# Layer 0 front: modulation products, value weights, value tiles and token sums placed differently

## The chip, the cores and the metric

The kernel runs on one core of a Trainium2 chip. The metric is device time in microseconds of one execution. The kernel is one straight program of 20932 profiled instructions; all five engines (TensorE or PE, VectorE or DVE, ScalarE or ACT, GpSimd or POOL, and SyncE or SP, which issues most transfers) work at once and meet by semaphores.

## What is computed

A two-layer encoder trunk on 1024 tokens of width 1024. Layer 0 is differential attention, layer 1 latent attention. Cut to what matters here:

```python
shift, scale, gate = split(silu(c) @ ada_w + ada_b)          # per layer: the modulation
h = rmsnorm(x, norm_g) * (1 + scale) + shift
q, k, v, z = split(h @ w_in0)                                 # layer 0, 8 heads
q, k = rope(q), rope(k)
p = softmax(q1 @ k1.T) - lam * softmax(q2 @ k2.T)
o = rmsnorm(p @ v, subln_g) * (1 - lam0) * silu(z)
x = x + gate * (o @ w_out0)
```

The modulation of layer 1 (shift and scale) depends on `c` alone, so its products can be done at any time before layer 1.

## The kernel before, in words

Float32 products are made from three matmuls: every operand is split into a rounded high part (a cast on ACT) and the rest (a subtraction on POOL or DVE), and `mm3` adds high*high, high*low and low*high in one accumulator. A weight block has 128 rows by 512 columns. All lines are those of the profile.

The front of layer 0 runs as follows.

1. The tokens are normalised, transposed and modulated into `h0`, first half, then second half (`h_chunk`, lines 519 and 782 to 793), and the value columns of heads 0 to 3 are made beside it. In the second half's loop, steps k = 1 to 4 each run one *modulation product* of layer 1: `mod_load` (L475) fetches 512 KB of weights, `mod_dot` (L480) multiplies by `c2` and sums along the row, on DVE. There are 16 such products: `MODS_K` (4) here, `sum(MODS)` (8) among the later value tiles, and the rest in attention 0.
2. `combos0` (L941 to L984) forms sums and differences of `h0`, the *token sums*, in 18 steps: additions on DVE, then a split into `TK` (cast on ACT L948, subtraction on DVE L949). Its last five steps make the fourth combination (L979, L980) and finish the splits. The steps hang on `side`, a list from which one entry is run at each tick, that is after each group of three matmuls; `None` is an empty tick. Beside it TensorE makes the second half of key and query strip 0 and gate strip 0 (`z_done`, whose output L851 frees the strip's accumulator).
3. For heads 2, 4 and 6 (`FRONT`), `z0_pair` makes a key strip and a query strip together with seven products instead of eight. Weights are fetched by `z0_fetch` (L932) a pair ahead, combined on DVE (L993 to L996) and split (`split_z`). After each output, `late(p, i)` starts work that belongs to what follows. In the last pair it fetches eight value weight blocks (`fetch_v1`, L1070, four and four) and splits them into `wv1` (`split_v1`, L1077 and L1078). Buffers: `zraw` has six, `zt` has twelve; both are freed by what last used them.
4. The first strip of `ORDER0` follows (`stream0.step(Z_PRE)`), then eight value tiles of heads 4 to 7 (`v0_tile`, "vps" in the profile). Each is stored with `store_v` (L418, L419, L421) from one of 16 `tk` buffers of the pool `tp`. Before tile `V_LATE` (6) attention begins with the first query tile.
5. Then `tp` is closed, and the pool `a0b` (the exponentials `e`, the transposed probabilities `pt`, the value tiles `vt`) takes its memory: each new tile waits for what lay there before.

Attention 0 goes over 8 heads, each in 8 query tiles (`q_tile`, `after_scores`). `stream0` fills TensorE with strips for later heads, and after each query tile `gate_step0` advances `gate_steps0` by one *slot*: its products (modulation, then eight for the gate) use two buffers `ada` of the pool `pg`. `rot_done` and `z_done` put a rotation's steps on `side`: `first_` and `second` on POOL, an empty tick, then `high` (cast on ACT, L398) and `low` (POOL).

The order on each engine is set by a planner at build time. It takes the program's order as priority and hoists instructions whose inputs and buffers it expects to be ready; some are tied by hand (`issue_after`, `keep_in_program_order`). Each engine and each queue then runs in that order.

Of the kernel before, what the change touches and what calls it, by code (L numbers as in the profile page):

```python
# [38 lines left out]
ROT = 2  # L39
# [4 lines left out]
Z_PRE = 16  # L44
V_LATE = 6
MODS = (2, 2, 2, 2, 0, 0, 0, 0)
MODS_K = 4
V1_AT = (3, 3)
NORM_AT = 5
PRE0 = (0, 0, 0, 0, 1, 2, 2, 3, 2, 2, 2)  # L50
# [3 lines left out]
FRONT = (2, 4, 6)  # L54
# [25 lines left out]
def f32v(ap):  # L80
    return ap.bitcast(F32)
# [3 lines left out]
def trunk(ctx: ExitStack, tc: tile.TileContext, A, out):  # L85
# [229 lines left out]
    side = Side()  # L315
# [100 lines left out]
    def store_v(l, sp, acc, tt, fh, tag="vst", bufs=None):  # L416
        v = sp.tile([P, 2, HF], F32R, name="tk" if tag == "tk" else "v_hl", tag=tag, bufs=bufs or VB[l])
        store_v.act = S.copy(v[:, 0, :], acc).ins  # L418
        V.tensor_sub(v[:, 1, :], acc, f32v(v[:, 0, :]))  # L419
        th, tl = tt // 4, tt % 4  # L420
        SP.dma_start(  # L421
            vS[l][fh][:, th, :, :, tl, :].rearrange("h p l d -> p l h d"),
            f32v(v).rearrange("p l (h d) -> p l h d", h=4),
        )

    def load_v(vp, l, h, ths=(0, 1)):
        vt = []
        for th in ths:
            t = vp.tile([P, 2, 4, P], F32R, name="vt", tag="vt", bufs=3)
            SP.dma_start(f32v(t), vS[l][h // 4][h % 4, th])  # L430
            vt.append(t)
        return vt
# [57 lines left out]
    def mod_job(n):  # L490

        j, i = divmod(n, 2)
        _, bsh, bsc, a_, b_ = mods[1]
        bias, acc = ((bsh, b_), (bsc, a_))[i]
        return A["ada_ss1"][j, i], bias[:, j : j + 1], acc[:, j : j + 1]

    def gen_mods(load, c2):

        for n in range(sum(MODS) + MODS_K):
            src, bias, acc = mod_job(n)  # L500
# [52 lines left out]
    pg = pool(stG, "pg")  # L553
# [228 lines left out]
    for k in range(KT + SKEW1):  # L782
        if k < KT:
            if 0 < k <= MODS_K:
                next(mods_g)
# [11 lines left out]
    def v0_tile(tt, fh, wv):  # L797
        half, tl = tt // 4, tt % 4
        acc = bank("acc", "vps")
        c_ = slice(tl * P, (tl + 1) * P)  # L800
        for k in range(KT):
            hh, hl = h0[k][half]
            mm3(acc, hh[:, c_], hl[:, c_], wv[k][0], wv[k][1], k == 0, k == KT - 1)
            side.tick()
        store_v(0, tp, acc, tt, fh, "tk", 16)


    KS, QS, GZ = {}, {}, {}
# [10 lines left out]
    def rot_done(kind, h):  # L819
        def f(acc, half):  # L820
            raw = wp.tile([P, HF], F32, name="rp_raw", tag="rp", bufs=6)
            if kind:
                S.copy(raw, acc)
            else:
                S.mul(raw, acc, SC0)
            fetch, *steps = rot_job(kind, h, half, G, raw)
            fetch()
            side.add(*[None] * ROT, *steps[:2], None, *steps[2:4])
        return f

    def load_k(h):
# [15 lines left out]
    def z_done(h):  # L847
        def f(acc, half):
            t = wp.tile([P, HF], F32, name="zth", tag="rp", bufs=6)
            S.activation(t, acc, AF.Tanh, scale=0.5)  # L850
            V.scalar_tensor_tensor(out=t, in0=t, scalar=1.0, in1=acc, op0=ALU.add, op1=ALU.mult)  # L851
            SP.dma_start(zS[h, half], t)
            if parked:
                fetch, *steps = rot_job(*parked.pop(0), G)
                side.add(fetch, None, None, *steps[:2], None, *steps[2:4])
        return f

    def load_gate(h, half):
# [58 lines left out]
    tp = pool(stT0, "tp", side="right")  # L917
# [8 lines left out]
    def zrt(name):  # L926
        return zp.tile([P, HF], F32, name=name, tag="zraw", bufs=6)

    def z0_fetch(p, parts):
        for m, f in parts:  # L930
            raw = zt("zraw") if p else zrt("zraw")
            SP.dma_start(raw, A["w_s0"][1 - m, FRONT[p], f])  # L932
            zraw.append(raw)
# [4 lines left out]
    def zt(name):  # L938
        return zp.tile([P, HF], F32, name=name, tag="zt", bufs=12)
# [124 lines left out]
    wv1 = []  # L1064
    wvraw = []

    def fetch_v1(n):
        for _ in range(n):
            raw = zrt("wvr")
            SP.dma_start(raw, A["w_v0"][len(wv1) + len(wvraw), 1])  # L1070
            wvraw.append(raw)

# [9 lines left out]
    zw = z0_weights()  # L1082
    zq = []
    cg = combos0()
    for _ in range(18):
        side.add(lambda: next(cg), None)
    for _ in gen_half(wk0, h0, 1, lambda acc: park(1, 0, 1.0)(acc, 1)):
        side.tick()
    wz0 = split_strip([(t, 4) for t in z0raw])
# [10 lines left out]
    def late(p, i):  # L1100
        if p + 1 < len(FRONT):
            if i < 2:
                z0_fetch(p + 1, ((i, 0), (i, 1)))
            return
        if i == 0:
            pre.extend(raw_of(*ORDER0[0], f) for f in range(2))
        if i == 1:
            fetch_v1(4)
        if i == 2:
            for _ in range(2):  # L1110
                for a, b in zip(w1, split_raw(pre.pop(0), 4)):
                    a += b
            split_v1(4, V)
            fetch_v1(4)
        if i == 3:
            split_v1(4, G)

# [63 lines left out]
    a0b = pool(st2b, "a0b")  # L1181
    for n, nb in (("osq", 4), ("o", 2)):
        a0b.tile([P, HF], F32, name=n, tag=n, bufs=nb)

# [89 lines left out]
            if kh == 1 and qp % 2 == 1:  # L1276
                c["close"](qp // 2, c["o_"], self.zz)

    tails, hooks, VT = [None, None], [], {}

    def run_tails(fill):

# [76 lines left out]
    def gate_steps0():  # L1359

        gcol = sm.tile([P, KT], F32, name="gcol", tag="gcol", bufs=1)
        yield
        w = []
        jobs = [mod_job(n) for n in range(sum(MODS) + MODS_K, 2 * KT)]
        late = len(jobs)
        jobs += [(A["ada_g0"][j], part("ada_bg0")[:, j : j + 1], gcol[:, j : j + 1]) for j in range(KT)]
        for n in range(len(jobs)):
            while len(w) < min(2, len(jobs) - n):
                with tc.issue_after(mod_load.last):
                    w.append(mod_load(jobs[n + len(w)][0], pg, 2))  # L1370
            yield
            if n >= late and (n - late) % 2 == 0:
                yield
            with behind("V"):
                mod_dot(w.pop(0), *jobs[n][1:], c2)
                if n == late - 1:
                    g, _, _, a_, _ = mods[1]
                    V.scalar_tensor_tensor(out=a_, in0=a_, scalar=1.0, in1=g, op0=ALU.add, op1=ALU.mult)
        SP.dma_start(gateS[0].rearrange("(p j) -> p j", p=P), gcol)
        yield  # L1380
        SP.dma_start(c2, gateS[0][None, :].to_broadcast([P, D]))
        gb = c2[:, :HF], c2[:, HF:]

        def two(name):
            t = pg.tile([P, D], F32, name=name, tag="ada", bufs=2)
            return t[:, :HF], t[:, HF:]

        def put(*pairs):
            for n, t in pairs:
                SP.dma_start(tS[0][n, h], t)  # L1390

        for h in range(4):
            b_ = (b11, b12), (b21, b22) = two("ob1"), two("ob2")
            for m in range(2):
                for f in range(2):
                    SP.dma_start(b_[m][f], A["w_out0"][f, 4 * m + h])
                yield
            for m in range(2):
                for f in range(2):
                    in_turn(G.tensor_mul(b_[m][f], b_[m][f], gb[f]))  # L1400
                if m:
                    put((0, b11))
                yield
            put((1, b21), (4, b22))
            in_turn(G.tensor_sub(b12, b12, b11))
            t2 = a0c.tile([P, HF], F32, name="ot2", tag="ot2", bufs=2)
            in_turn(G.tensor_sub(t2, b22, b12))
            yield
            put((3, b12), (2, t2))
            in_turn(G.tensor_sub(b11, t2, b11))  # L1410
            in_turn(G.tensor_sub(b21, b21, t2))
            yield
            put((5, b11), (6, b21))
            yield
        for h, wait in ((0, 46), (1, 54)):
            while slot0 < wait:
                yield
            a_ = (a11, a12), (a21, a22) = two("oa1"), two("oa2")
            for m in range(2):
                for f in range(2):  # L1420
                    SP.dma_start(a_[m][f], oF[0][h + 4 * f, m])
                yield
            for _ in combine(a11, a12, a21, a22):
                yield
            SP.dma_start(sS[0][0, h], a22)
            SP.dma_start(sS[0][2, h], a21)
            yield
            SP.dma_start(sS[0][1, h], a11)
            SP.dma_start(sS[0][3, h], a12)
            yield  # L1430
# [36 lines left out]
    class Seven:  # L1467
# [40 lines left out]
        def fetch(self, n):  # L1508
            for h in range(4):
                self.fetch_a(n, h)  # L1510
                self.fetch_w(n, h)
# [13 lines left out]
    class Pre2:  # L1525
        n = 0
# [304 lines left out]
    for n, rows, acc, f in ((3, 4, Z, 1), (4, 0, Z, 1), (5, 4, Y, 1), (6, 4, Y, 0)):  # L1831
# [5 lines left out]
        for i in range(4):  # L1837
# [24 lines left out]
            if i == 1 and n == 5:  # L1862
                raws = [[], []]
                with tc.issue_after(w6):
                    for k, (tag, nb) in enumerate((("wraw", 2), ("gz", 3))):
                        for f in range(2):
                            raw = wst.tile([P, HF], F32, name="wraw", tag=tag, bufs=nb)
# [796 lines left out]
    for tiles, a, b in LAST1:  # L2664
        acc = {i: bank("z", "oyb") if a else Y[i] for i in tiles}
# [87 lines left out]
```

## Time and profile before

| | us |
|---|---|
| median of 3 runs (lowest, highest) | 1413.85 (1412.5, 1414.33) |
| the profiled execution | 1414.53 |
| its span, first to last instruction | 1412.7 |
| PE busy | 1368.7 |
| DVE busy | 999.6 |
| ACT busy | 736.7 |
| POOL busy | 716.5 |

In rows of a timeline the first number is the start in us from the span's start, the second the length in us, followed by engine, line, operation, the tile written, the tiles read, and a count; a bracket at the end tells how long the engine had been idle and whom it waited for. In rows of waits stand the waiting engine, tile and line, whom it waited for, the total in us, how many times, and the longest.

### The profile page before, as it was taken

How to read it: one execution, taken by the hardware profiler on the slowest of the kernel's cores; microseconds unless marked ns; L12 is line 12 of the kernel's file. 1: busy time of each engine (PE TensorE's matmuls, PEld its weight loads, DVE VectorE, ACT ScalarE, POOL GpSimd, SP SyncE). 2: the span in 40 equal slices, each digit the busy share in tenths (PEclk: the TensorE clock that was granted, in tenths of full speed). 3: DMA queues.
4: the chain of work that ended last, by engine and by line, in shares of the span. 5: the costliest groups of instructions: out<-in, count | busy, mean ns of one | idle time of the engine just before them, and what ended most of it. 6: DMA issues, size and time to landing. Idle time of an engine off the chain costs nothing.

```text
span 1412.7 us, 20932 instructions
## 1 busy us (share of the span) xinstructions
PE 1368.7 (97%) x7298; PEld 1144.2 (81%) x7298; DVE 999.6 (71%) x1414; ACT 736.7 (52%) x1332; POOL 716.5 (51%) x574
## 2 busy tenths in 40 slices
PE   8998889899999999999999999999999999999997
PEld 6786678788888888887787788887888888888886
DVE  7799726899877878788687986545656655555684
ACT  5534313556666556566756543335444454445554
POOL 4434441466688776454785233433141273844673
PEclk9999999999999999999999999999999999999999
DMA  9854788786878787756584236399434354665473
GB/s 338 280 172 156 247 227 258 222 241 192 256 236 245 222 246 223 226 163 202 161 290 155 79 106 221 124 299 265 148 107 117 107 181 147 196 218 198 147 258 120
DMA packets 175243, 282.41 MB, mean 200 GB/s; under 512 B 23457, under 2 KB 60449, under 8 KB 175138
## 3 DMA queue, kind: packets, MB, share of 16 engines
q1 hardware_dynamic: 168610, 266.40, 60.8%
q10 hardware_dynamic: 4608, 8.39, 1.6%
q0 software_dynamic: 1920, 6.29, 1.1%
q8 instruction: 57, 0.93, 0.3%
q14 instruction: 48, 0.39, 0.1%
HBM read 182.49 MB, written 86.98 MB: 191 GB/s over the span
## 4 chain that ended last, share of the span: by engine, by line
PE 68%; DVE 11%; DMA 6%; issue 5%; ACT 4%; POOL 4%; SPq 2%; POOLq 0%; ACTq 0%; DVEq 0%
PE s L2367 8%; PE tr L439 6%; PE s L1155 6%; PE acc L180 6%; PE acc L179 6%; PE acc L178 6%; PE pv L178 3%; PE pv L180 3%; PE pv L179 3%; DVE ada L480 2%; PE vps L178 1%; PE vps L180 1%; PE vps L179 1%; PE oy L179 1%; PE oy L180 1%
## 5 line engine op out<-in xcount | busy, mean ns | idle before, releaser
L442 DVE TENSOR_TENSOR ptl<-tr,pth 128x512 fp32r<-128x512 f32 x256 | 176.1, 688 | 148.9 <-ACT pth L441 144.4
L441 ACT CAST pth<-tr 128x512 fp32r<-128x512 f32 x256 | 150.3, 587 | 249.8 <-PE tr L439 243.5
L456 DVE TENSOR_REDUCE nm<-s 128x1 f32<-128x1024 f32 x192 | 233.6, 1217 | 22.1 <-PE s L1155 13.0
L224 POOL TENSOR_TENSOR wl<-wraw,wh 128x512 fp32r<-128x512 f32 (+2 forms) x65 | 85.3, 1314 | 250.2 <-ACT wh L223 182.6
L458 ACT ACTIVATE e<-s,nm 128x1024 f32<-128x1024 f32 x128 | 143.4, 1120 | 52.0 <-DVE nm L456 50.1
L439 PE MATMUL tr<-ident,e 128*128 128x128 f32 x1024 | 156.0, 274 | 8.3 <-DVE ptl L442 7.8
L439 PEld LDWEIGHTS tr<-ident,e 128*128 128x128 f32 x1024 | 121.0, 141 | 49.4 <-DVE ptl L442 25.6
L178 PE MATMUL pv<-pth,vt 128*128 128x256 f32 x512 | 147.5, 288 | 0.0
L179 PE MATMUL pv<-ptl,vt 128*128 128x256 f32 x512 | 146.8, 287 | 0.0
L180 PE MATMUL pv<-pth,vt 128*128 128x256 f32 x512 | 144.6, 282 | 0.0
L178 PE MATMUL acc<-h0h,wh 128*128 128x512 f32 x264 | 109.8, 416 | 3.4 <-ACT wh L223 3.4
L180 PE MATMUL acc<-h0h,wl 128*128 128x512 f32 x264 | 105.7, 401 | 4.6 <-POOL wl L224 4.6
L179 PE MATMUL acc<-h0l,wh 128*128 128x512 f32 x264 | 104.8, 397 | 0.0
L178 PEld LDWEIGHTS pv<-pth,vt 128*128 128x128 f32 x512 | 97.5, 190 | 2.9 <-ACT pth L441 0.2
L179 PEld LDWEIGHTS pv<-ptl,vt 128*128 128x128 f32 x512 | 97.5, 190 | 2.5
L180 PEld LDWEIGHTS pv<-pth,vt 128*128 128x128 f32 x512 | 97.5, 190 | 0.5
L1503 POOL TENSOR_TENSOR wol<-wol,woh 128x512 fp32r<-128x512 f32 x56 | 82.4, 1495 | 25.4 <-ACT woh L1502 23.8
L1155 PE MATMUL s<-ks,qa 128*128 128x512 f32 x256 | 85.4, 414 | 5.1 <-DVE e L1163 4.9
L1163 DVE SCALAR_TENSOR_TENSOR e<-s,z,e 128x1024 f32<-128x1024 f32 x64 | 82.2, 1284 | 2.0
L1155 PE MATMUL s<-ks,qb 128*128 128x512 f32 x256 | 83.1, 400 | 0.0
L458 ACT ACTIVATE s<-s,nm 128x1024 f32<-128x1024 f32 x64 | 70.1, 1095 | 6.6 <-DVE nm L456 6.6
L224 POOL TENSOR_TENSOR wl<-zraw,wh 128x512 fp32r<-128x512 f32 (+2 forms) x32 | 42.8, 1346 | 50.5 <-ACT wh L223 50.5
(494 smaller groups left out, 3612.5 us busy)
## 6 DMA issues: line engine op xcount, KB each, us to landing
ada<-in_ada_ss SPq DMA_DIRECT2D x32, 512.0 KB, 5.6
vt<-vS SPq DMA_DIRECT2D x32, 512.0 KB, 5.0
wol<-tS SPq DMA_DIRECT2D x56, 256.0 KB, 5.3
wraw<-in_w_s SPq DMA_DIRECT2D x52, 256.0 KB, 3.8
vS<-v_hl SPq DMA_DIRECT2D x24, 512.0 KB, 5.8
tS<-ob SPq DMA_DIRECT2D x48, 256.0 KB, 3.7
bc_s<-bc_d SPq DMA_DIRECT2D x34, 256.0 KB, 4.1
hS<-rp_sw ACTq DMA_DIRECT2D x32, 256.0 KB, 4.8
```

Of the source, the lines that this page charges most:

```text
L178: PE.matmul(psum, ah, bh, start=first, stop=False, skip_group_check=skip)
L179: PE.matmul(psum, ah, bl, start=False, stop=False, skip_group_check=skip)
L180: mm3.last = PE.matmul(psum, al, bh, start=False, stop=last, skip_group_check=skip).ins
L224: sub = (V if pair_of else G).tensor_sub(l_[:, :n], raw[:, :n], f32v(h_[:, :n]))
L439: transpose_p.last = PE.transpose(tr[:, j, :], p[:, kt * P : (kt + 1) * P], ident).ins
L441: mk["S"] = S.copy(pth[kh][:, :, dst], tr).ins
L442: mk["V"] = V.tensor_sub(ptl[kh][:, :, dst], tr, f32v(pth[kh][:, :, dst])).ins
L456: mk["V"] = V.reduce_max(nm, s_ps, axis=AX.X, negate=True).ins
L458: mk["S"] = S.activation(e, s_ps, AF.Exp, bias=nm, scale=1.0, accum_out=zs).ins
L1155: PE.matmul(s_ps[:, kc * HF : (kc + 1) * HF], src[:, c, ql], KS[h][kc][:, c, :], start=fst, stop=not fst)
L1503: sub = eng.tensor_sub(lo, raw, f32v(hi))
L2367: PE.matmul(s_ps[:, kc * HF : (kc + 1) * HF], lhs, rhs(kc), start=i == 0, stop=i == 4)
```

## The change

- `MODS_K` goes from 4 to 0: the four modulation products of the second half's loop are no longer there. The last four of the 16 products used to be in `gate_steps0`; now the last eight are. Four empty slots that stood between the gate's products go, so that the list has as many slots as before.
- `fetch_v1` takes the buffers from which it fetches. The first four value weights are fetched at the end of the pair before the last, into `zraw`; the other four in the last pair, into `zt`.
- Value tiles 6 and 7 are stored from the two `ada` buffers of `pg` instead of two `tk` buffers of `tp`.
- The value tiles of head 0 are loaded right after `a0b` opens, ahead of its other tiles, instead of at their first use.
- The last five steps of `combos0` stand four ticks apart instead of two.
- Each rotation has two empty ticks ahead of `high` instead of one.

```diff
-MODS_K = 4
+MODS_K = 0
 ...
-        store_v(0, tp, acc, tt, fh, "tk", 16)
+        store_v(0, *((tp, acc, tt, fh, "tk", 16) if tt < V_LATE else (pg, acc, tt, fh, "ada", 2)))
 ...
-            side.add(*[None] * ROT, *steps[:2], None, *steps[2:4])
+            side.add(*[None] * ROT, *steps[:2], None, None, *steps[2:4])
 ...
-                side.add(fetch, None, None, *steps[:2], None, *steps[2:4])
+                side.add(fetch, None, None, *steps[:2], None, None, *steps[2:4])
 ...
-    def fetch_v1(n):
+    def fetch_v1(n, home):
         for _ in range(n):
-            raw = zrt("wvr")
+            raw = home("wvr")
 ...
-    for _ in range(18):
-        side.add(lambda: next(cg), None)
+    for i in range(18):
+        side.add(lambda: next(cg), *[None] * (1 if i < 13 else 3))
 ...
             if i < 2:
                 z0_fetch(p + 1, ((i, 0), (i, 1)))
+            if i == 3 and p + 2 == len(FRONT):
+                fetch_v1(4, zrt)
             return
 ...
         if i == 1:
-            fetch_v1(4)
+            fetch_v1(4, zt)
         if i == 2:
 ...
             split_v1(4, V)
-            fetch_v1(4)
 ...
     for n, nb in (("osq", 4), ("o", 2)):
         a0b.tile([P, HF], F32, name=n, tag=n, bufs=nb)
+    VT = {0: load_v(a0b, 0, 0)}
 ...
-    tails, hooks, VT = [None, None], [], {}
+    tails, hooks = [None, None], []
 ...
             yield
-            if n >= late and (n - late) % 2 == 0:
-                yield
             with behind("V"):
                 mod_dot(w.pop(0), *jobs[n][1:], c2)
```

## The prediction

> **What bounds the kernel now.** I read the page's busy shares first, then busy time by stretches, then the waits of TensorE and the queues, then the timelines of the stretches where TensorE stands still.
>
> ```profile
> PE 1368.7 (97%) x7298; PEld 1144.2 (81%) x7298; DVE 999.6 (71%) x1414; ACT 736.7 (52%) x1332; POOL 716.5 (51%) x574
> 0.00:73.00 73.00, 67.43 (x302) 52.19 (x303) 53.31 (x93) 41.45 (x70) 33.83 (x33) 1.00 0.90 310
> 73.00:185.00 112.00, 98.42 (x414) 78.92 (x413) 103.77 (x138) 42.54 (x75) 49.85 (x31) 0.95 0.60 192
> 185.00:250.00 65.00, 65.00 (x293) 53.82 (x292) 25.20 (x37) 16.21 (x28) 12.91 (x11) 1.00 0.86 239
> 250.00:270.00 20.00, 16.99 (x89) 13.54 (x87) 17.86 (x23) 11.96 (x22) 7.93 (x6) 0.91 0.82 237
> 270.00:330.00 60.00, 58.06 (x334) 48.51 (x333) 54.68 (x83) 36.49 (x65) 37.76 (x33) 1.00 0.79 231
> 330.00:400.00 70.00, 69.66 (x408) 59.43 (x407) 58.39 (x85) 44.19 (x79) 49.16 (x42) 1.00 0.73 219
> ```
>
> The first line is the page's summary; the rest give, for each stretch, its length, then busy time of PE, PEld, DVE, ACT and POOL with counts, granted clock, DMA share and GB/s. TensorE sets the pace nearly everywhere. In the front, from 73 to 185, it does not: DVE is busy 103.77 of 112.00 us and TensorE loses 13.6 us and clock. From 185 to 250 TensorE is full and DVE is not, so time won before 185 is kept if the inputs come earlier too. Where the losses are:
>
> ```profile
> PE zacc L178 <- DVE zth L851: 5.0, 1, 5.0
> PE acc L180 <- POOL wl L224: 4.0, 2, 3.1
> PE acc L178 <- ACT wh L223: 3.4, 1, 3.4
> 92.00:112.00 20.00, 20.00 (x90) 16.57 (x89) 20.00 (x31) 10.92 (x19) 3.07 (x2) 1.00 0.49 162
> 114.90:120.00 5.10, 0.12 (x2) 0.03 (x1) 5.10 (x8) 1.93 (x4) 1.50 (x2) 0.96 0.12 34
> 120.00:123.30 3.30, 3.30 (x9) 2.64 (x10) 3.30 (x3) 0.34 (x1) 3.27 (x2) 0.55 0.53 179
> 169.70:190.50 20.80, 13.42 (x50) 9.85 (x49) 14.83 (x20) 4.73 (x8) 10.91 (x7) 0.84 0.84 267
> ```
>
> At full pace a matmul of this kind takes 20.00 / 90 = 0.222 us. Stall one is 5.0 us of standing still at 114.9, and then nine matmuls in 3.30 us where 2.0 would do (clock 0.55): 6.3 us. Stall two is the first strip after the last pair: 50 matmuls in 20.80 us where 11.1 would do: 9.7 us, of which 7.4 are the waits on ACT and POOL and the rest the clock.
>
> **The change part by part.**
>
> *Four products out of the front, 73 to 80.* Their rows, with DVE's next work and the two late outputs:
>
> ```profile
> 73.10 1.27 DVE L480 CUSTOM_DVE_ANT_0 ada<-ada,c,vec 128x1024 f32<-128x1024 f32 x1
> 74.30 2.31 DVE L480 CUSTOM_DVE_ANT_0 ada<-ada,c,vec 128x1024 f32<-128x1024 f32 x1
> 76.54 2.30 DVE L480 CUSTOM_DVE_ANT_0 ada<-ada,c,vec 128x1024 f32<-128x1024 f32 x1
> 78.77 1.27 DVE L480 CUSTOM_DVE_ANT_0 ada<-ada,c,vec 128x1024 f32<-128x1024 f32 x1
> 79.97 0.68 DVE L961 TENSOR_TENSOR tc<-h0h,h0l 128x512 f32<-128x512 f32 x1
> 113.39 3.45 DVE L979 TENSOR_TENSOR t2f<-h0h,t2f 128x512 f32<-128x512 f32 x2
> 119.18 0.67 DVE L851 SCALAR_TENSOR_TENSOR zth<-zth,acc 128x512 f32<-128x512 f32 x1
> 107.38 0.59 ACT L850 ACTIVATE zth<-acc 128x512 f32<-128x512 f32 x1
> SPq L932 <- DVE moda L480: 13.5, 1, 13.5
> ```
>
> The four hold DVE from 73.10 to 79.97, 6.87 us, and DVE then has no idle time until stall one ends (20.00 of 20.00 busy above). L851, the gate of z strip 0, frees the accumulator that the stalled product needs; its tanh was ready at 107.97, and it waited only for its turn on DVE. With 6.87 us less ahead of it, it ends at 119.85 - 6.87 = 112.98, before TensorE asks at 114.9: 1.9 us to spare. The first pair's weight fetches (L932, on SP) also lose a wait of 13.5 us for these products, whose buffers lay in the same memory. I take 6.0 of the 6.3 us. Ends: 0, if DVE cannot use the gap because its sums wait for buffers; 6.3.
>
> *Token sums spread.* The last five steps of `combos0` (L979, L980, L949) come four ticks apart instead of two. At L979 two sums took 3.45 us in front of L851; this moves them behind it. Same stall, so nothing more is counted. The fourth combination is needed only in the seventh product (tick 56 of the front's list; its last step moves from 34 to 42), eight ticks after stall one's product; price if late: a wait no longer than stall one.
>
> *Value weights sooner.* What delays stall two's weights:
>
> ```profile
> 170.04 1.74 DVE L1078 TENSOR_TENSOR tk<-wvr,tk 128x512 fp32r<-128x512 f32 x1
> 172.30 1.88 DVE L1078 TENSOR_TENSOR tk<-wvr,tk 128x512 fp32r<-128x512 f32 x3
> 171.81 1.53 SPq L1070 DMA_DIRECT2D wvr<-in_w_v x2
> 175.32 1.32 ACT L1077 CAST tk<-wvr 128x512 fp32r<-128x512 f32 x2 [7.15 <-DMA wvr<-in_w_v]
> 176.55 0.61 ACT L223 CAST wh<-wraw 128x512 fp32r<-128x512 f32 x1
> 176.01 3.98 POOL L1078 TENSOR_TENSOR tk<-wvr,tk 128x512 fp32r<-128x512 f32 x2 [4.79 <-ACT tk L1077]
> 179.96 3.48 POOL L224 TENSOR_TENSOR wl<-wraw,wh 128x512 fp32r<-128x512 f32 x2
> 165.34 1.93 DVE L480 CUSTOM_DVE_ANT_0 ada<-ada,c,vec 128x1024 f32<-128x1024 f32 x1 [3.46 <-DMA ada<-in_ada_ss]
> ```
>
> Six `zraw` buffers serve eight value weights, so the last two are fetched at 171.81, once DVE has split earlier ones. ACT stands 7.15 us for them with the strip's cast (L223) behind; POOL then does two value splits before the strip's (L224). In the changed kernel the first four come a pair earlier into `zraw`, the other four into `zt`, which has twelve buffers. Nothing needs splitting before a fetch, and the ACT wait goes. The 8 fetches on SP are the same eight. What is late next is POOL: four value splits and two strip splits remain in its order, so I leave the smallest wait of today's three, 0.9 us (4.0 less 3.1), plus one of POOL's 1.3 to 2.0 us: 9.7 - 3.2 = 6.5 us gained. Ends: 0 and 9.7; below nothing only by the rival on ACT. With four `zt` buffers held, outputs of the last pair (`zv`, `zu5`, `z22`) may wait for an older tile's split or store; I take 0, since stores and splits of pair one lie some 19 us back (7 products of 12 matmuls); if that cover is gone it is part of that rival.
>
> *Last two value tiles in the `ada` buffers, head 0's value load moved up.*
>
> ```profile
> 239.24 0.68 DVE L403 TENSOR_TENSOR rp_raw<-rp_r,rp_sw 128x512 fp32r<-128x512 f32 x1
> 245.53 0.27 DVE L1162 TENSOR_SCALAR z<-z,zz,neglam 128x1 f32<-128x1 f32 x1 [3.05 <-ACT e L458]
> 244.30 1.11 ACT L458 ACTIVATE e<-s,nm 128x1024 f32<-128x1024 f32 x1
> 240.38 1.25 SPq L421 DMA_DIRECT2D vS<-tk x1
> DMA to landing us min/median/max: 3.6/3.7/6.9
> PE s L1155 <- DVE e L1163: 3.2, 4, 1.8
> ```
>
> The second attention tile's exponential starts at 244.30 although its maximum was ready at 239.24 (when DVE went on to L403): `e` lies where value tiles 5 and 6 wait for their stores, the last issued at 240.38, landing 3.7 us later. DVE idles 3.05 us there, and from 250 to 270 TensorE lacks 3.0 us and 9% of clock (1.8): 4.8. With tiles 6 and 7 elsewhere, and `vt` taking those places, `e` lies on earlier tiles and starts up to 5 us sooner. DVE stays behind for other reasons, so I take 2.0; ends 0 and 4.8. The two value loads now wait on SP for tile 5's store; behind them queue tiles 6 and 7, key loads and strip weights. Cost taken 0, end +3.7 (one landing). The first gate fetch can start only when tiles 6 and 7 are stored, about 244, and lands near 250; today's first product there runs at 254.8: covered.
>
> *Four products into attention 0.* Twelve products with four empty slots become sixteen in as many slots; what follows keeps its slot. Four fetches of 512 KB leave SP at 60 and join it here: 2.1 MB, about 9 us at the 231 GB/s above, into stretches with 21 to 27% of DMA time free.
>
> ```profile
> L480 DVE CUSTOM_DVE_ANT_0 ada<-ada,c,vec x24: 1269/1467/2324, 73.1 to 363.5; 128x1024 f32<-128x1024 f32 x24
> 283.90 1.28 DVE L1163 SCALAR_TENSOR_TENSOR e<-s,z,e 128x1024 f32<-128x1024 f32 x1
> 333.45 2.09 DVE L480 CUSTOM_DVE_ANT_0 ada<-ada,c,vec 128x1024 f32<-128x1024 f32 x1
> ```
>
> The empty slots are near 284, 304, 327 and 348. In 330 to 400 TensorE is full (69.66 of 70) although four products run there, so the last two hide; in 270 to 330 DVE has 5.3 us left and TensorE waits for its `e` (3.2 us from 250 to 400, the row above), so the first two cost their length. I take +2.5 (2 x 1.27); ends 0 and 9.3 (4 x 2.32).
>
> By the Trainium skill ("SBUF — State Buffer", "Who interferes with whom") a DVE instruction with two SBUF inputs and a POOL instruction that reads SBUF exclude each other for a whole instruction. The trace agrees: the product takes 1.27 us alone and 2.3 beside POOL. By that rule all four would come out near the long form here, since POOL is busy 37.76 of 60 us, and the sum would be 2.1 us worse in the two that count.
>
> *One more empty tick before the rotations' cast.* ACT no longer stands for L394; keys and queries are stored one step (0.68 us) later, loaded slots later. Taken as 0.
>
> **Sum.** -6.0 - 6.5 - 2.0 + 2.5 = -12.0 us. The profiled execution took 1414.53 us (span 1412.7, 1.8 us around it), 0.7 above the median 1413.85: 1402.5 against the profile, 1402 for the median.
>
> **Rivals.** (a) Value weights come early but stall two stays, because DVE, still late, waits for `ada` fetches (3.46 us at 165.34) and for what SP holds back: -6.0 - 2.0 + 2.5 = -5.5, 1408. For: eight products stay there. Against: those fetches waited for stores of a DVE that is now 6.87 us less behind. (b) DVE paces heads 0 and 1 with products of 2.32 us: +9.3, and no gain at the exponential: -3.2, 1410.7. For: 54.68 of 60 busy. Against: TensorE full from 330. By the Trainium skill's rule above this is the likelier of the prices for a product. (c) Slower: the earlier casts (L1077) stand ahead of pair two's weight casts on ACT and wait in order for fetches or buffers, so that stall two is merely split: it stays, and a second of the same price, 9.7, comes inside pair two: -5.5 + 9.7 = +4.2, 1418. It decides from 5.5 us on. For: exactly this wait of 7.15 us exists today. Against: the fetches no longer need splits. (d) The instruction order is planned anew, stalls move, the time stays: 1411 to 1417. (e) All goes, and the products hide: 6.3 + 9.7 + 4.8 = -20.8, 1393.
>
> **How the numbers follow.** Forecast 0.55 (1398 to 1406), (a) 0.15, (b) 0.10, (c) 0.10, (d) 0.04, (e) 0.06. Within 0.2%, about what a measurement of this kernel can tell from no change, means 1411.0 to 1416.7: faster 0.82 (forecast, a, e, half of b), same 0.08, slower 0.10. Leaving out (e) at one end, and (c) and most of (d) at the other, gives 1396 to 1412.5.
>
> **What would show it.** Right: no product between 73 and 80; no wait of PE on L851; no wait of ACT L1077 on `wvr`; the first strip after the pairs in 11 to 14 us; first scores near 213 instead of 225; the second tile's exponential within 2 us of its maximum; sixteen products in heads 0 and 1 with TensorE's loss there up by less than 3 us. Wrong: a new wait of PE in pair one or two, or first scores early and the end not.

## The result, and the profile after

The changed kernel is slower: 1422.26 us median (1416.48 to 1424.95, 8 runs) against 1412.39 (1409.68 to 1415.26, 8 runs) of the kernel before beside it, ratio 1.0060 with an interval of 1.0038 to 1.0082. The forecast was 1402, its range ended at 1412.5. Ratios compare the means of the executions, so they need not equal the quotient of the medians. Here 0.001 of a ratio is 1.4 us. The profiled execution took 1416.81 us (span 1414.9), among the quickest of this kernel, so its trace shows only 2.2 of the 8.5 us. The traces say where time goes; how much is taken from the ratios.

The first line is the page's summary of the changed kernel, the others its stretches (columns as in the prediction), first the five that answer to those of before:

```profile
PE 1369.7 (97%) x7298; PEld 1141.1 (81%) x7298; DVE 1010.1 (71%) x1414; ACT 734.5 (52%) x1332; POOL 721.1 (51%) x574
73.00:185.00 112.00, 102.85 (x429) 81.84 (x428) 100.27 (x129) 42.61 (x76) 50.47 (x32) 0.97 0.57 187
185.00:250.00 65.00, 65.00 (x304) 53.60 (x303) 31.81 (x46) 18.91 (x33) 16.09 (x14) 1.00 0.84 251
250.00:270.00 20.00, 18.71 (x103) 15.05 (x102) 17.21 (x24) 11.38 (x20) 9.86 (x8) 1.00 0.73 222
270.00:330.00 60.00, 56.83 (x321) 46.92 (x320) 56.86 (x78) 34.10 (x61) 37.21 (x31) 1.00 0.80 233
330.00:400.00 70.00, 65.13 (x379) 54.41 (x377) 63.18 (x87) 42.73 (x77) 46.00 (x39) 1.00 0.78 235
110.00:120.00 10.00, 9.61 (x43) 7.63 (x42) 10.00 (x13) 3.96 (x8) 3.52 (x3) 1.00 0.34 112
480.00:545.00 65.00, 61.39 (x346) 51.65 (x345) 46.70 (x70) 36.37 (x66) 38.75 (x34) 0.97 0.73 226
```

The front is better, by 4.4 us of TensorE work between 73 and 185. But 330 to 400, where TensorE had been full, now lacks 4.9 us, and 480 to 545, which no step of the prediction names, lacks 3.6 us and some clock. The same two places in the kernel before, with the whole of heads 1 and 2 as one row:

```profile
300.00:420.00 120.00, 119.22 (x694) 101.45 (x692) 102.64 (x149) 73.59 (x130) 86.22 (x73) 1.00 0.76 232
480.00:545.00 65.00, 65.00 (x378) 55.75 (x377) 50.47 (x74) 40.72 (x72) 42.64 (x37) 1.00 0.84 248
```

So three questions stand: why the front gives so little, what heads 1 and 2 lose, and what happens near 500. The waits of TensorE from 60 to 200 and DVE's products in the changed kernel answer the first:

```profile
PE zacc L180 <- POOL wl L224: 4.6, 7, 1.4
PE acc L180 <- POOL wl L224: 2.8, 1, 2.8
PE zacc L178 <- ACT wh L223: 1.7, 1, 1.7
119.41 1.27 DVE L480 CUSTOM_DVE_ANT_0 ada<-ada,c,vec 128x1024 f32<-128x1024 f32 x1
123.99 1.27 DVE L480 CUSTOM_DVE_ANT_0 ada<-ada,c,vec 128x1024 f32<-128x1024 f32 x1
134.30 2.32 DVE L480 CUSTOM_DVE_ANT_0 ada<-ada,c,vec 128x1024 f32<-128x1024 f32 x1
137.75 1.27 DVE L480 CUSTOM_DVE_ANT_0 ada<-ada,c,vec 128x1024 f32<-128x1024 f32 x1
127.71 0.62 ACT L398 CAST rp_sw<-rp_r 128x512 fp32r<-128x512 f32 x1 [6.65 <-DVE rp_r L394]
128.23 0.61 ACT L223 CAST wh<-zraw 128x512 fp32r<-128x512 f32 x1
120.00:140.00 20.00, 16.63 (x64) 12.61 (x63) 20.00 (x26) 6.10 (x12) 9.21 (x6) 0.91 0.60 197
```

Stall one is gone. But the planner put four of the eight later products into 119 to 140, where the kernel before had two (136.7 and 139.6). DVE is busy all 20 us, as before, and the order on ACT is another. These are the same two casts in the kernel before:

```profile
124.86 0.62 ACT L223 CAST wh<-zraw 128x512 fp32r<-128x512 f32 x1
128.63 0.62 ACT L398 CAST rp_sw<-rp_r 128x512 fp32r<-128x512 f32 x1 [3.15 <-DVE rp_r L394]
```

The rotation's sum (L394) comes no later than before, at 127.00 instead of 127.92. But ACT now stands 6.65 us for it with the weight cast (L223) behind, which had gone first, and POOL's splits and TensorE follow. The waits for `zacc` add up to 6.3 us in the changed kernel and to 6.2 before, 5.0 of them stall one. Counted from the first product of a pair to that of the next, pair one takes 20.7 us instead of 25.7, pair two 24.7 instead of 19.9, and pair three, up to the strip, 22.1 instead of 20.2.

### The profile page after: what moved, and what is told of

The parts are those of the page before. It is cut to its first block, busy times and chain, and to the rows that moved or that the text cites. A ratio compares the mean times of both kernels' runs of the same rounds, so it can differ in the third digit from the quotient of the medians.

```text
span 1414.9 us, 20936 instructions
## 1 busy us (share of the span) xinstructions
PE 1369.7 (97%) x7298; PEld 1141.1 (81%) x7298; DVE 1010.1 (71%) x1414; ACT 734.5 (52%) x1332; POOL 721.1 (51%) x574
## 4 chain that ended last, share of the span: by engine, by line
PE 71%; DVE 13%; DMA 4%; issue 4%; ACT 4%; POOL 3%; SPq 1%; POOLq 0%; DVEq 0%; ACTq 0%
PE s L2367 10%; PE tr L439 7%; PE acc L180 7%; PE acc L179 6%; PE acc L178 6%; PE s L1156 6%; PE pv L179 4%; PE pv L178 4%; PE pv L180 4%; DVE ada L480 2%; DVE nm L456 2%; DVE e L1164 2%; PE zacc L180 1%; PE zacc L178 1%; PE zacc L179 1%
## 5 line engine op out<-in xcount | busy, mean ns | idle before, releaser
L458 ACT ACTIVATE e<-s,nm 128x1024 f32<-128x1024 f32 x128 | 143.5, 1121 | 63.8 <-DVE nm L456 63.2
L1156 PE MATMUL s<-ks,qa 128*128 128x512 f32 x256 | 85.6, 415 | 7.4 <-DVE e L1164 7.1
L1156 PE MATMUL s<-ks,qb 128*128 128x512 f32 x256 | 83.0, 399 | 3.4 <-DMA qb<-hS 3.4
L1164 DVE SCALAR_TENSOR_TENSOR e<-s,z,e 128x1024 f32<-128x1024 f32 x64 | 82.1, 1283 | 1.8
L458 ACT ACTIVATE s<-s,nm 128x1024 f32<-128x1024 f32 x64 | 70.0, 1094 | 13.7 <-DVE nm L456 13.7
L224 POOL TENSOR_TENSOR wl<-zraw,wh 128x512 fp32r<-128x512 f32 (+2 forms) x32 | 46.1, 1447 | 52.3 <-ACT wh L223 40.1
```

The costliest lines, as they stand in the source:

```text
L224: sub = (V if pair_of else G).tensor_sub(l_[:, :n], raw[:, :n], f32v(h_[:, :n]))
L458: mk["S"] = S.activation(e, s_ps, AF.Exp, bias=nm, scale=1.0, accum_out=zs).ins
L1156: PE.matmul(s_ps[:, kc * HF : (kc + 1) * HF], src[:, c, ql], KS[h][kc][:, c, :], start=fst, stop=not fst)
L1164: combined.append(V.scalar_tensor_tensor(out=e0, in0=e1, scalar=z1[:, 0:1], in1=e0, op0=ALU.mult, op1=ALU.add).ins)
```

## The experiments

"Fetch" stands for the earlier value weights, "tiles" for the last two value tiles in the `ada` buffers with head 0's value load, "sums" for the token sums, "products" for `MODS_K` with the slots, "tick" for the extra empty tick. Each kernel was timed beside runs of the kernel before. The results first:

| | run | median us | ratio to before | interval |
|---|---|---|---|---|
| all five again | e1 | 1420.97 | 1.0060 | 1.0043 to 1.0077 |
| products | e2 | 1416.92 | 1.0041 | 1.0028 to 1.0055 |
| all but products | e3 | 1421.62 | 1.0065 | 1.0053 to 1.0078 |
| all five, four products left out | e4 | 1416.90 | 1.0031 | 1.0020 to 1.0043 |
| fetch | e5 | 1409.87 | 0.9982 | 0.9973 to 0.9992 |
| tiles | e6 | 1409.50 | 0.9980 | 0.9968 to 0.9991 |
| sums | e7 | 1413.39 | 1.0009 | 0.9999 to 1.0019 |
| tick | e8 | 1421.34 | 1.0072 | 1.0056 to 1.0089 |
| all but tick | e9 | 1416.33 | 1.0035 | 1.0023 to 1.0048 |
| fetch, tiles | e10 | 1406.50 | 0.9961 | 0.9949 to 0.9972 |
| fetch, tiles, sums | e13 | 1408.17 | 0.9971 | 0.9958 to 0.9983 |
| fetch, tiles, tick | e14 | 1418.97 | 1.0037 | 1.0024 to 1.0050 |
| fetch, tiles, products | e15 | 1416.24 | 1.0030 | 1.0019 to 1.0040 |
| all but sums | e16 | 1420.27 | 1.0049 | 1.0035 to 1.0063 |
| all five, one query load sooner | e17 | 1416.00 | 1.0019 | 1.0005 to 1.0033 |
| tick, one query load sooner | e18 | 1419.35 | 1.0038 | 1.0024 to 1.0051 |

**Is it the products?** e1 is the changed kernel; e2 has only its first and last hunk, e3 all the others. e4 is the changed kernel with four products not computed (their fetches stay):

```diff
-                mod_dot(w.pop(0), *jobs[n][1:], c2)
+                if n in (4, 7, 10, 13):
+                    w.pop(0)
+                    V.memset(jobs[n][2], 0.0)
+                else:
+                    mod_dot(w.pop(0), *jobs[n][1:], c2)
```

> The changed kernel once more, for a profile of a typical execution (the first one, 1416.8 us, was among its quickest). Theory A (the four products paid for in attention 0): first value tile about 187 us, as in the first profile, and the loss in heads 0 and 1, 6 to 10 us against the kernel before. Theory B (the loss lies elsewhere and later): heads 0 and 1 as before, another stage longer. Ratio 1.004 to 1.008 in either.

> The kernel before with only the four products moved into attention 0 (and the empty slots gone). Theory A: stall one shrinks, the front is 2 to 5 us shorter, attention 0 6 to 10 us longer: slower by 2 to 8 us. Theory B (each edit only makes the planner lay the instructions differently, and the loss is not the products'): within 4 us of before, with no more loss in heads 0 and 1 than before.

> The changed kernel with the four products back in the front and the empty slots back. Theory A: heads 0 and 1 take what they took before (235 to 357 us, 122 us), so 4 to 10 us faster than the changed kernel, and at or below the kernel before. Theory B: still 4 us or more above the kernel before.

> The changed kernel; four of the sixteen products of attention 0, those in the slots that were empty before, are left out and a small memset stands in their place (their fetches stay, so part of the modulation and gate is not computed). Theory A: heads 0 and 1 lose their 6 to 10 us again, 1412 us or less. Theory B: no more than 4 x 1.3 = 5 us of DVE time go and TensorE does not move: within 2 us of the changed kernel.

The products alone cost 5.8 us, and four fewer give 4.1 back. But e3, without the moved products, is as slow as the whole, so they are not the only cause. Heads 0 and 1, from the first weights of head 0 to those of head 2, take 122.4 us before, 128.9 in e1, 119.2 in e3 and 119.5 in e4: this stage recovers as Theory A had it, but in e3 the time does not, and in e4 head 4 to head 5 takes 68.0 us instead of 58.0. What a product costs shows in heads 1 and 2. Stretch and group of DVE's products in the changed kernel, then in e4, then the group (240 to 420) of before:

```profile
300.00:420.00 120.00, 112.82 (x645) 94.05 (x643) 108.37 (x150) 69.38 (x124) 84.03 (x71) 1.00 0.78 235
L480 DVE CUSTOM_DVE_ANT_0 ada<-ada,c,vec 128x1024 f32<-128x1024 f32 x16 | 27.2, 1701 | 0.3 <-DMA ada<-in_ada_ss 0.3
```

```profile
300.00:420.00 120.00, 117.29 (x680) 99.25 (x679) 101.53 (x150) 73.16 (x131) 84.43 (x73) 1.00 0.80 241
```

```profile
L480 DVE CUSTOM_DVE_ANT_0 ada<-ada,c,vec 128x1024 f32<-128x1024 f32 x12 | 18.8, 1565 | 0.0
```

Sixteen products take 27.2 us where twelve took 18.8: 8.4 us more, or 2.1 for each one added. Not all of them stretch: eleven of the sixteen take 1.27 or 1.28 us, and one takes 4.07. TensorE loses 6.4 of 119.22 us there; with the four left out, 1.9.

**Which edit, one by one.**

```diff
+            if i == 3 and p + 2 == len(FRONT):      # e5, with fetch_v1(4, zt)
+                fetch_v1(4, zrt)
+    VT = {0: load_v(a0b, 0, 0)}                     # e6, with store_v(... pg, "ada")
+        side.add(lambda: next(cg), *[None] * (1 if i < 13 else 3))           # e7
+            side.add(*[None] * ROT, *steps[:2], None, None, *steps[2:4])     # e8, and in z_done
```

> The kernel before with only the value weights' fetches moved (four at the end of the pair before the last, four into the twelve buffers). Theory A (the forecast's step): ACT no longer waits 7 us for the last two, the first strip after the pairs shortens from 20.8 to about 14 us, 4 to 7 us faster. Theory B (one part of the rest is to blame for the 9 us of e3, and it is this one): 5 us slower or more.

> The kernel before with only the last two value tiles in the other buffers and head 0's value load moved up. Theory A: the second attention tile's exponential no longer waits for stores, 1 to 3 us faster. Theory B (this part is to blame for e3): the order of attention 0's instructions is laid anew from its first tile on, 5 us slower or more, lost in attention 0.

> The kernel before with only the last five token sums spread. Theory A: stall one loses its two long sums, 0 to 4 us faster. Theory B (to blame for e3): 5 us slower or more.

> The kernel before with only the second empty tick ahead of each rotation's cast. Theory A: nothing, within 1.5 us. Theory B (to blame for e3): keys and queries are stored later, TensorE or the loads wait for them in attention 0, 5 us slower or more.

Fetch and tiles gain 2.5 and 2.8 us, the sums are nothing that can be told, and the tick, one empty step of a list, costs 10.2 us (8.5 by the medians, the figure that later expectations use). Fetch stays below its 4 to 7 us: the first strip shortens from 20.8 to 18.7 us only, with a wait of 4.7 us for POOL left in it. Lines of attention lie one or two lower in some kernels: L1155 here is L1156 in the changed kernel. TensorE's waits between 180 and 700 that the kernel before has not (line, releaser, total, times, longest), SP's largest between 230 and 660, and below them the same SP row of before:

```profile
PE s L1155 <- ACT e L458: 5.3, 2, 3.2
PE s L1155 <- DMA qb<-hS: 3.6, 1, 3.6
SPq L464 <- POOL rq_y L1239: 43.1, 11, 8.4
```

```profile
SPq L464 <- POOL rq_y L1239: 24.7, 8, 6.4
```

L464 stores the reciprocal roots that POOL makes at the end of a head (`bcast_rows`). SP issues in order, so what stands behind it waits too. L844 loads a head's queries as the tiles `qa` and `qb`. SP's timeline with the tick, then before, at head 2 to 3 and at head 4 to 5:

```profile
405.31 0.33 SPq L464 DMA_DIRECT2D bc_d<-rq_y  x1
406.15 0.43 SPq L383 DMA_DIRECT2D rp_raw<-rS  x1
525.55 0.33 SPq L464 DMA_DIRECT2D bc_d<-rq_y  x1
525.99 0.58 SPq L844 DMA_DIRECT2D qb<-hS  x1
```

```profile
399.83 0.42 SPq L383 DMA_DIRECT2D rp_raw<-rS  x1
405.98 0.37 SPq L464 DMA_DIRECT2D bc_d<-rq_y  x1
512.27 1.23 SPq L844 DMA_DIRECT2D qb<-hS  x2
521.50 0.33 SPq L464 DMA_DIRECT2D bc_d<-rq_y  x1
```

With the tick a rotation's store (`low`) is one step later in the program, and in the order that comes out L464 has passed ahead of the parked rotation's fetch (L383) and of part of the next head's query load (L844). At head 2 to 3 ACT and TensorE show what follows the late fetch; with the tick, then before:

```profile
415.14 0.62 ACT L398 CAST rp_sw<-rp_r 128x512 fp32r<-128x512 f32 x1 [4.53 <-POOL rp_r L394]
416.17 1.11 ACT L458 ACTIVATE e<-s,nm 128x1024 f32<-128x1024 f32 x1 [0.40 <-ACT rp_sw L398]
417.42 0.73 PE L1155 MATMUL s<-ks,qa 128*128 128x512 f32 x2 [3.24 <-ACT e L458]
```

```profile
410.85 1.12 ACT L458 ACTIVATE e<-s,nm 128x1024 f32<-128x1024 f32 x1
411.95 0.61 ACT L398 CAST rp_sw<-rp_r 128x512 fp32r<-128x512 f32 x1
```

The rotation's cast (L398) now stands ahead of the exponential (L458) on ACT and waits 4.53 us there; before, the exponential went first. From this came the theory of the following runs: it is the order on SP.

**In company, and with the store elsewhere.** e9 is the changed kernel with one tick taken back, e10 has fetch and tiles alone. e11 (with the tick) and e12 (without) send the store of L464 to POOL's own queue:

```diff
-        SP.dma_start(d_.rearrange("(p t) -> p t", p=P), y)
+        eng.dma_start(d_.rearrange("(p t) -> p t", p=P), y)   # eng=G from L1191
```

> The changed kernel with only the extra empty tick taken back. Theory (the tick, through the order of SP's queue, carries the loss and the parts add): 8.5 us less than the changed kernel's 1421 to 1422, so 1412 to 1414 (ratio to before 0.999 to 1.001), and in attention 0 no wait of PE on the query load (3.4 to 3.6 us with the tick). Rival (the products saturate DVE and with the re-planned front carry most of it, the tick costs little once they are there): 1418 to 1421, ratio 1.004 to 1.006.

> Before with only the earlier value weights and the last value tiles in other buffers (with the early value load); no products moved, no extra tick, token sums as before. Theory (the parts add): -2.9 - 3.3 = -6.2 us, 1406.5 (ratio 0.9956). Rival (both win the same idle time in front of attention 0, or the win is taken back by a stall that moves): -3 us, 1409.7 (ratio 0.998).

> Before with the extra empty tick, and with the store of the reciprocal roots in layer 0 (L464) issued from POOL's own DMA queue, so that SP never stands for it. Theory (the tick costs because SP stands at that store with a query load and a parked fetch behind it): at most 2 us slower than the same kernel without the tick (e12), and no wait of PE on qb in attention 0. Rival (the tick costs because the rotations' stores themselves come later, whatever stands on SP): 6 to 9 us slower than e12.

> Before with only that store moved to POOL's DMA queue: the control of e11. Theory: SP loses 24.7 us of waits that cost TensorE nothing in the kernel before, so no change within 2 us, 1411 to 1415. Rival: the issue takes POOL about a microsecond 16 times, beside its busy stretches: 2 to 6 us slower.

e9 fell between its two theories: in company the tick costs 3.5 us, not 10.2, and without it TensorE still waits 3.4 us for a query load (`qa`). e10 came out as the sum of its parts. e12 took 1422.1 us (1.0068, 1.0056 to 1.0080), slower than either of its theories had it, and e11 1431.07 (1.0135, 1.0122 to 1.0148). SP's largest wait from 230 to 700 in e12:

```profile
SPq L466 <- DMA bc_d<-rq_y: 47.3, 14, 11.3
```

The load of L466 on SP now stood for the same store's landing. The wait had moved, not gone; whether that is what makes e12 slow was not tried. e11 speaks against the order on SP as the tick's whole price. TensorE waits for no query load in its attention 0, and yet the tick costs 9.5 us there, nearer to the rival's 6 to 9 than to the theory's 2. From head 2 to head 3 e11 takes 65.8 us and e12 57.2, although L383 goes out at 404.22 in e11, ahead of L466 at 412.09.

**The missing corners.** Products, tick and sums, each on top of fetch and tiles, and the whole without the sums:

> Before with the earlier value weights, the last value tiles in other buffers, and the token sums spread; no products moved, no extra tick. Theory (the sums cost nothing here either; products and tick each spoil the same gain): 1407 (ratio 0.996 to 0.997). Rival (the sums, which alone cost 0.6 us, are what turns the gain around once the front has moved): 1413 to 1416, so that 7 to 9 us of the loss are theirs.

> Before with the earlier value weights, the last value tiles in other buffers, and the extra empty tick. Theory (the tick alone carries the whole step from 1406.5 to the 1421.6 that these with the sums took): 1419 to 1422. Rival (additive, 8.5 us for the tick): 1415. Second rival (it costs only together with the sums): 1407 to 1410.

> Before with the earlier value weights, the last value tiles in other buffers, and the four products moved into attention 0; no extra tick, sums as before. Theory (the products cost more once the front has moved, since they take the slots in which the value tiles' gain lay): 1414 to 1417. Rival (additive, 4.4 us): 1411. Second rival (the loss needs the sums): 1407 to 1409.

> The changed kernel with only the token sums put back two ticks apart. Theory (the sums are nothing): 1420 to 1422, as the changed kernel. Rival (they carry a part): 1412 to 1416.

From 0.9961, the tick costs 0.0076 (10.7 us), the products 0.0069 (9.7), both together 0.0088 (12.4), the sums 0.0010 (1.4, within the intervals). Tick and products mostly pay for the same thing. The first weights (L1164) of head 4 and of head 5 show what, in fetch and tiles (e10), then in the changed kernel:

```profile
466.24 1.28 DVE L1164 SCALAR_TENSOR_TENSOR e<-s,z,e 128x1024 f32<-128x1024 f32 x1
...
525.86 1.28 DVE L1164 SCALAR_TENSOR_TENSOR e<-s,z,e 128x1024 f32<-128x1024 f32 x1
```

```profile
473.49 1.28 DVE L1164 SCALAR_TENSOR_TENSOR e<-s,z,e 128x1024 f32<-128x1024 f32 x1
...
537.51 1.28 DVE L1164 SCALAR_TENSOR_TENSOR e<-s,z,e 128x1024 f32<-128x1024 f32 x1
```

Eight tiles take 59.6 us in the one and 64.0 in the other. With the store on SP, all traces with the tick, or with the products on top of fetch and tiles (the changed kernel, e1, e3, e4, e8, e9, e14, e15, e16), have 63.6 to 68.0 us here, and SP has one stand of 8.1 to 10.2 us at L464 near 520. Before and in e2, e5, e6, e7, e10 and e13 it is 57.9 to 59.6 us, and no such wait there is over 6.5. Products alone (e2) do not flip the order; with the front moved they do, also without the tick (e9, e15: TensorE waits 3.4 and 3.9 us for `qa`). e11, with the store on POOL, has 64.4 us without any of these waits.

**The place itself.** One number changed, in the changed kernel (e17) and in the kernel with the tick alone (e18):

```diff
-        if h < NH - 1 and i == 5 + (h + 1) % 2:
+        if h < NH - 1 and i == 5 + (h + 1) % 2 - (h == 4):
             load_q(h + 1, 0)
```

> The changed kernel with one number changed: in head 4 the load of the next head's first queries is asked for one attention tile sooner, so that on SP it stands ahead of the store L464 that waits for POOL, and not behind it. All else, POOL's order included, is the same but for some lines around that place. Theory (this one place carries the 6 us that every kernel with the tick, or with the products on top of fetch and tiles, loses from head 4 to head 5): no wait of PE on qb there (3.2 to 3.4 us now), the stretch from head 4's first weights to head 5's back from 64 to 58 to 59 us, and 1415 to 1417 in all, 5 us less than the changed kernel. Rival (the wait is only one sign of engines that are late anyway, and another takes its place): 1419 to 1422.

> Before with the extra empty tick and the same query load one attention tile sooner. Theory: the tick's 8.5 us fall to 2.5 to 3.5 (what is left is the parked fetch behind L464 from head 2 to head 3), 1415 to 1416. Rival (the tick's cost lies in the later stores of keys and queries as such): 1419 to 1421.

SP, and the wait of TensorE, in the changed kernel; then SP in e17, with its stretch:

```profile
510.89 1.34 SPq L844 DMA_DIRECT2D qa<-hS  x2
521.47 0.33 SPq L464 DMA_DIRECT2D bc_d<-rq_y  x1
521.90 0.58 SPq L844 DMA_DIRECT2D qb<-hS  x1
529.97 1.10 PE L1156 MATMUL s<-ks,qb 128*128 128x512 f32 x2 [3.41 <-DMA qb<-hS]
```

```profile
508.94 1.32 SPq L844 DMA_DIRECT2D qa<-hS  x2
510.37 1.22 SPq L844 DMA_DIRECT2D qb<-hS  x2
522.04 0.32 SPq L464 DMA_DIRECT2D bc_d<-rq_y  x1
480.00:545.00 65.00, 64.79 (x376) 55.02 (x375) 50.84 (x73) 39.77 (x72) 43.12 (x38) 1.00 0.87 249
```

The store leaves at the same time, but the query load is 11.5 us earlier, TensorE's wait is gone, and head 4 to 5 takes 58.7 us. The ratio falls from 1.0060 to 1.0019 (5.8 us), with the intervals apart: the order on SP is the cause at this place. With the tick alone it falls from 1.0072 to 1.0038 (4.8 us). More is left than was expected (5.4 us, not 2.5 to 3.5), and the median, 1419.35, lies in the rival's range: head 2 to 3 still takes 63.4 us there against 57.2 before. The waits shown for that place are there too (ACT 5.62 us, TensorE 4.34), but moving its fetch was not tried, and e11 loses there with its fetch ahead. So the order on SP is shown for head 4 to 5, and the rest of the tick's cost stays open.

The best of all these is e10, fetch and tiles alone, 0.9961 of before: 5.5 us faster, and 0.99 of the changed kernel.

## Why the prediction was wrong

The step that failed most is "One more empty tick before the rotations' cast", "Taken as 0". It costs 10.2 us alone, 10.7 on top of fetch and tiles, 3.5 where the products have flipped the order already. The prediction itself said that "keys and queries are stored one step (0.68 us) later, loaded slots later"; it did not look at what stood on SP near those loads. The row was there: SP stands 24.7 us at L464 in the kernel before, and TensorE waits for no query load there. With the order flipped a part of the query load goes out 11.5 us later, not 0.68, and that place is worth 5.8 us. Nor does it hold that "ACT no longer stands for L394": in e8 it still waits 25.8 us for it in all, 33.9 before, and one of these waits stands in front of an exponential.

*Products into attention 0, +2.5 (ends 0 and 9.3).* On top of fetch and tiles 9.7 us, net of what they give the front, which is little: e10, with the four products still in it, reaches its first value tile at 187.0, the changed kernel at 186.7. The step that failed is "In 330 to 400 TensorE is full (69.66 of 70) although four products run there, so the last two hide": it was full with DVE at 58.39 of 70 us, and with DVE at 63.18 it has 65.13. Slack on DVE over the whole stretch was no cover. The price was mis-sized too: four products add 8.4 us of DVE time, where 1.27 us was counted for two and nothing for two. By the rule of the Trainium skill ("SBUF — State Buffer", "Who interferes with whom") the prediction had put all four near the long form of 2.3 us. The trace agrees that the two engines hold each other up, as each of the five longer products began while a POOL instruction ran; it does not give the long form for all, as eleven of the sixteen stay at 1.27 or 1.28 us. A part of the 9.7 us is the order on SP (head 4 to 5 takes 65.1 us in e15, 59.6 in e10); how the rest divides was not measured.

*Stall one, -6.0.* The stall went nearly as worked out: L851 ended at 113.69 (forecast 112.98), no product stood between 73 and 80, TensorE was busy 9.61 us from 110 to 120, and pair one became 5.0 us shorter. But the planner filled DVE's gap at once, and pairs two and three became 4.8 and 1.9 us longer. This is the mechanism of rival (d), an order planned anew, which had 0.04; the sign named under "Wrong", a new wait of PE in pair one or two, is there (1.70 and 1.02 us in pair two).

*Stall two, -6.5.* The first strip after the pairs took from 171.10 to 186.7, 15.6 us instead of 20.8, with one wait of 2.80 us left, for POOL: 5.2 us gained, though outside the 11 to 14 that was named. ACT's waits for `wvr` fell to 1.4 us in all, from one of 7.15, and rival (c) did not come. What was late next was POOL's order, as said, and it costs more than the 3.2 us that were left for it: fetch alone leaves a strip of 18.7 us. Together the front gave 3.8 us (190.5 to 186.7), not 12.5, and first scores came at 221.4 instead of near 213. Fetch alone, timed, is worth 2.5 us, so the term of 6.5 was too large.

*Attention start, -2.0.* Right: the second tile's later exponential starts at 238.08, 0.17 us after its maximum, and tiles alone gain 2.8 us.

*Token sums, 0.* Right within the intervals. But "Same stall" hides an exchange: spread alone (e7), the sums take TensorE's wait for L851 from 5.0 to 0.9 us, and its other waits for `zacc` grow from 1.2 to 8.0.

The chances counted as faster (forecast, (a), (e) and half of (b)) add up to 0.81, not 0.82, which changes nothing.

The waits that were to go went or shrank. What was not priced is what the planner does with the room, on DVE and on SP.

## What to carry to other kernels

An in-order issue queue is a resource with an order of its own: before a step is moved by a slot, list which loads stand near a store that waits for an engine, and what TensorE needs from behind it. A move that empties a busy engine under a planner is only worth what the planner does not pull into the gap, so read the engine's stretch after it, and expect late items to be hoisted. Time parts of a mixed change by themselves and in company: here two of five parts carried the gain and two others paid for the same stall, so that removing one of those alone gave back nothing (the products) or 3.5 of 8.5 us (the tick).

## What the runs showed of the hardware

In these traces SP issues its transfers in order, so a load can stand behind one small store (128x4 values) whose source is late: 8.8 us in the changed kernel. Issued 11.5 us later than in e17, that load cost TensorE 3.41 us of standing, and the next matmuls were slower (L1156 `qb` pairs 1.10 us instead of 0.62); with the load ahead of the store the kernel is 5.8 us faster (e17). Moving such a store to another queue did not take the wait off SP while the load that reads it stayed there: from 230 to 700 SP then stood 47.3 us for L466 (e12) instead of 34.8 for L464 before, and the kernel was slower (1.0068).
